# Feed-forward output product of an encoder layer: weight sums formed a product ahead, product ends in small pieces, last product closed row tile by row tile

## The chip, the core and the metric

The kernel runs on one core of one Trainium2 chip. The core has TensorE (matrix products), VectorE and ScalarE (elementwise work), GpSimd, and a sync engine whose only work here is to issue transfers. The metric is the device time of one execution in microseconds (us). The kernel before takes 2346.46 us, the median of three runs; the fastest of them took 2345.99 us and one was disturbed (10064.24 us).

## The reference

The layer has a mixer (stick-breaking attention, a spatial-gating branch and memory attention) and a feed-forward part, for 1024 prompt rows and 64 sample rows of width 1024. The change touches only the second product of the feed-forward part, the norm behind it and the residual sum:

```python
D_FF = 2816
def ffn_sublayer(x, g_pre, w_ffn_in, w_ffn_out, g_post):
    a, b = jnp.split(rmsnorm(x, g_pre) @ w_ffn_in, 2, axis=-1)
    return x + rmsnorm((jax.nn.silu(a) * b) @ w_ffn_out, g_post)
```

`rmsnorm(y, g)` divides each row by the root of its mean square and multiplies it by g, so a row of the output is final only when both of its column halves are known.

## The kernel before

All matrix products are float32 products made of three TensorE passes: each operand is split into a high part (a rounded copy, `fp32r`) and a low part (the difference), and `mm3` adds high·high, high·low and low·high.

The product `h @ w_ffn_out` (1088 x 2816 by 2816 x 1024) is done by Strassen's scheme in its seven-product form. The 2816 rows of the weight are two halves of eleven blocks of 128 rows (index k, `NK = 11`), and its 1024 columns are two halves of 512. `FO[0, k]` holds the two column halves of block k of the upper half, `FO[1, k]` those of the lower half; each is a tile `fw` of 128 x 2 x 512. The seven products are run one after the other in the order p1, p2, p3, p5, p6, p7, p4. Each takes eleven steps k. A step needs one operand pair: the weight operand W (a block of the weight, or a sum of blocks) and the activation operand A (a block of h, or a sum, which earlier code has stored in device memory as `fS` or `fA` and which is loaded into a tile `fa`). `fsplit` makes the pair W, W-low, and the pair A, A-low, in tiles `fop`: one ScalarE copy for the high part, one VectorE subtraction for the low part. So a step has two ScalarE copies and two VectorE subtractions.

With the pairs of step k, TensorE does 12 matmuls of 128 x 512 (`fout_mm`): two pairs of row tiles, `jp` 0 and 1, two row tiles each, three passes each. The sums of a `jp` stand in one two-bank tile `pb` of the accumulator memory; there are three such tiles. p1, p2, p3 and p5 have two more matmuls a step for the 64 sample rows (`fout_sample`).

In p5, p6, p7 and p4 the weight operand is itself a sum: `fout_ops` forms it in place in a `fw` tile with one more VectorE subtraction right before `fsplit` (before.py L1242 to L1249). In that step the ScalarE copy waits for the sum, and the VectorE subtraction waits for the copy.

At the end of a product `fout_post` (L1344) takes the sums out of `pb` and combines them with stored ones (tiles `p1`, `p3`, `p5`, `C11`, 128 x 2 x 512 each; the profile's views leave digits away, so that the tiles p1, p3 and p5 all read `p` there, and C11 reads `C`). After p6 the four row tiles 0 to 3 are complete in both column halves, after p7 the right halves of row tiles 4 to 7, after p4 their left halves. `scaled` (L1337) then takes a ScalarE square sum of each row tile and half (`square`, output `junk`) and multiplies by the gain `gpf` on VectorE. When both halves of a row tile have their square sums, two tiny VectorE instructions and one on GpSimd make `rstd`, and two VectorE instructions SCALAR_TENSOR_TENSOR ("puts") add the scaled halves onto the residual `x2r`, which is loaded from device memory; each is stored by a transfer.

What sets the order: the kernel is written out by hand through a planner that runs while the program is built. `get_wop(i)` writes out operand pairs up to `LA[0]` operands ahead of the one that TensorE takes (`LA_END = 4`: two steps), and their loads `RA[0]` further. Each engine executes its own list in that order. `fout_post` is written out in the step that ends the product, so the operands of steps k = 0 and 1 of the next product stand ahead of it on VectorE and those of k = 2 behind it. Small background pieces (`stream`) are taken by `breathe()` when the planner's clock of their engine is no more than `BACK[0]` us (`BACKLOG_END = 6`) ahead of TensorE's. The sync engine issues all transfers in order; a store waits there for the instruction that makes its data, and loads behind it wait too.

The last product, `fout_last` (L1399), does all eleven steps for row tiles 4 and 5 (`jp` 0, six matmuls a step), keeps the operands, and then does row tile 6 and row tile 7 with 33 matmuls each. `last_tile` finishes a row tile.

Of the kernel before, what the change touches and what calls it, by code (L numbers as in the profile page):

```python
# [15 lines left out]
P = 128  # L16
# [28 lines left out]
LA_FIN = 2  # L45
LA_END = 4
RA_END = 4

FS_GATE = [2, 9]
LA_BR = 4  # L50
# [1 line left out]
BACKLOG_ATT = 1000  # L52
BACKLOG_MEM = 6
BACKLOG_OUT = 10
BACKLOG_END = 6
X_AHEAD = 4
AHEAD = 4

# [86 lines left out]
def encoder_layer(  # L145
# [14 lines left out]
    clock, at = clocks.t, clocks.at  # L160
# [40 lines left out]
    def f32(ap):  # L201
        return ap.bitcast(F32)
# [10 lines left out]
    def act(out, in_, f=AF.Copy, **kw):  # L213
        nc.scalar.activation(out, in_, f, **kw)

    def sub(out, a, b):
        nc.vector.tensor_tensor(out, a, b, op=ALU.subtract)

    def add(out, a, b):
        nc.vector.tensor_tensor(out, a, b, op=ALU.add)  # L220

    def mul(out, a, b):
        nc.vector.tensor_tensor(out, a, b, op=ALU.mult)
# [152 lines left out]
    def get_raw(i):  # L376
        return raw_t[i]
# [827 lines left out]
    def w_raw(h, m, k):  # L1205

        def f():
            if (h, k) not in FO:
                FO[h, k] = A([P, 2, 512], F32, "fw")
            load(FO[h, k][:, m], w_ffn_out[0, (h * NK + k) * P:(h * NK + k + 1) * P, m * 512:(m + 1) * 512])  # L1210
            return FO[h, k][:, m]
        raws.append(f)
        return len(raws) - 1

    def a_raw(name, k):
        def f():
            until(lambda: (name, k) in STORED)
            x = U([P, 512], F32, "fa")
            load(x, fS[name][k])
            return x  # L1220
        raws.append(f)
        return len(raws) - 1

    def fsplit(src):
        t = A([P, 2, 512], F32R, "fop")
        act(t[:, 0], src)
        sub(t[:, 1], src, f32(t[:, 0]))
        return t

    FORM = {"p1": "A11", "p2": "A12", "p3": "S4", "p5": "S1", "p6": "S2", "p7": "S3", "p4": "A22"}  # L1230

    def fout_ops(name, k):


        new = {"p1": (0, 0), "p2": (1, 0), "p3": (1, 1), "p5": (0, 1)}
        r = [w_raw(*new[name], k)] if name in new else []
        ra = a_raw(FORM[name], k)

        def w():
            if name in ("p1", "p2", "p3"):  # L1240
                return fsplit(get_raw(r[0]))
            t, b = FO[0, k], FO[1, k]  # L1242
            x, y = {"p5": (t[:, 1], t[:, 0]), "p6": (b[:, 1], t[:, 1]), "p7": (t[:, 0], b[:, 1]),
                    "p4": (b[:, 0], b[:, 1])}[name]
            if name == "p7":
                sub(x, y, x)
            else:
                sub(x, x, y)
            return fsplit(x)  # L1249
        return wop(w, *r), wop(lambda: fsplit(get_raw(ra)), ra)  # L1250


# [43 lines left out]
    def square(j, m, src):  # L1296

        n = src.shape[0]
        ss = sm.tile([P, 1], F32, tag="ssf", name=nm("ssf"), bufs=18)[:n]
        act(U([P, 512], F32, "junk")[:n], src, AF.Square, accum_out=ss)  # L1300
        SQ.setdefault(j, {})[m] = (ss, src)
        if len(SQ[j]) == 2:
            s0, s1 = SQ[j][0][0], SQ[j][1][0]
            add(s0, s0, s1)
            SQ[j]["r"] = rstd_of(s0, D)
            n_ = n

            def ld():
                x = RES[j] = A([P, D], F32, "x2r")[:n_]
                load(x, x2sc[j * P:j * P + n_])  # L1310

            def put(m):
                src = SQ[j][m][1]
                x = RES[j][:, m * 512:(m + 1) * 512]
                nc.vector.scalar_tensor_tensor(x, src, SQ[j]["r"], x, op0=ALU.mult, op1=ALU.add)

            def out(m):
                x = RES[j][:, m * 512:(m + 1) * 512]
                store(y_prompt[0][j * P:(j + 1) * P, m * 512:(m + 1) * 512] if j < 8 else
                      y_sample[0][:, m * 512:(m + 1) * 512], x)  # L1320
            need = ("dve", lambda: max(at(RES[j], SQ[j]["r"]), at(SQ[j][0][1], SQ[j][1][1])))
            st = [x for m in range(2) for x in ((*need, lambda m=m: put(m)),
                                                ("sync", lambda: at(RES[j]), lambda m=m: out(m)))]
            if j in RES:
                stream(*st)
            else:
                stream(("sync", lambda: 0, ld), *st)
# [6 lines left out]
    def pair(pt):  # L1334
        return pt.rearrange("p (i n) -> p i n", i=2)

    def scaled(j0, m, c):  # L1337

        for i in range(2):
            square(j0 + i, m, c[:, i])  # L1340
        g = FO["g"][:, m * 512:(m + 1) * 512]
        mul(c, c, g.unsqueeze(1).to_broadcast([P, 2, 512]))

    def fout_post(name, jp, pt):  # L1344
        def new(key):
            FO[key, jp] = A([P, 2, 512], F32, key)
            return FO[key, jp]

        src = pair(pt)
        if name in ("p1", "p3"):  # L1350
            act(new(name), src)
        elif name == "p2":
            add(new("C11"), src, FO["p1", jp])
        elif name == "p5":
            act(new("p5"), src)
            c = FO["p3", jp]
            add(c, src, c)
        elif name == "p6":
            t, c = FO["p1", jp], FO.pop(("p3", jp))
            add(t, src, t)  # L1360
            add(c, c, t)
            scaled(2 * jp, 0, FO.pop(("C11", jp)))
            scaled(2 * jp, 1, c)
        elif name == "p7":
            t, c = FO["p1", jp], FO.pop(("p5", jp))
            add(t, src, t)
            add(c, c, t)
            scaled(4 + 2 * jp, 1, c)

    def last_tile(j, pt):  # L1370
        u = FO["p1", j // 2][:, j % 2]
# [27 lines left out]
    def fout_last():  # L1399

        kept = []

        def first(k, ws):
            def f(tiles):
                w, a = tiles
                kept.append((w, a))
                if k == 0:
                    fill(psum_free("b"))
                    FO["pt", 0] = PB()
                fill(at(w, a))  # L1410
                fout_mm(FO["pt", 0], a, w, 0, (0, 1), k)
                breathe()
                if k == NK - 1:
                    for j in range(2):
                        last_tile(j, FO["pt", 0])
            steps.append((ws, f))

        def rest(j):
            def f(tiles):
                if j == 2:  # L1420
                    fill(psum_free("b"))
                    FO["pt", 1] = PB()
                res_early(4 + j)
                for k, (w, a) in enumerate(kept):
                    fout_mm(FO["pt", 1], a, w, 1, (j,), k)
                    if k % 3 == 2:
                        breathe()
                last_tile(j, FO["pt", 1])
            steps.append(([], f))
        for k in range(NK):  # L1430
            first(k, fout_ops("p4", k))
        for j in (2, 3):
            rest(j)

    for name in ("p1", "p2", "p3", "p5", "p6", "p7"):
# [609 lines left out]
```

## Time and profile before

| what | before |
|---|---|
| median of the runs shown | 2346.46 us |
| the profiled execution's own time | 2345.06 us |
| its span, first to last instruction | 2343.1 us |
| TensorE busy / weight loads busy | 95% / 92% of the span |
| VectorE busy / ScalarE busy | 68% / 33% |
| mean granted clock of TensorE | 0.986 of full speed |
| start of p6 (its first matmul) | 2204.18 us |
| end of the last matmul | about 2335.5 us |

The profile is one execution. Times are microseconds from the start of the span. PE is TensorE's matmuls, PEld its weight loads, DVE VectorE, ACT ScalarE, POOL GpSimd, SP the sync engine. PEclk is the granted TensorE clock as a share of 2.4 GHz. A matmul's end is modelled, so the starts are the better measure. In the timeline, a row of TensorE merges matmuls that follow each other, and the bracket says how long the engine stood idle ahead of it, and what ended that.

### The profile page before, as it was taken

How to read it: one execution, taken by the hardware profiler on the slowest of the kernel's cores; microseconds unless marked ns; L12 is line 12 of the kernel's file. 1: busy time of each engine (PE TensorE's matmuls, PEld its weight loads, DVE VectorE, ACT ScalarE, POOL GpSimd, SP SyncE). 2: the span in 40 equal slices, each digit the busy share in tenths (PEclk: the TensorE clock that was granted, in tenths of full speed). 3: DMA queues.
4: the chain of work that ended last, by engine and by line, in shares of the span. 5: the costliest groups of instructions: out<-in, count | busy, mean ns of one | idle time of the engine just before them, and what ended most of it. 6: DMA issues, size and time to landing. Idle time of an engine off the chain costs nothing.

```text
span 2343.1 us, 40746 instructions
## 1 busy us (share of the span) xinstructions
PE 2229.2 (95%) x16465; PEld 2146.5 (92%) x16465; DVE 1602.8 (68%) x2473; ACT 783.3 (33%) x1383; POOL 141.8 (6%) x236
## 2 busy tenths in 40 slices
PE   7899999999999999988899999988999999999986
PEld 6899999999999998877799999987999999988764
DVE  7856688867776665699934354488777777764676
ACT  8432222332222224667612122243121112143442
POOL 2000000000000000243200000221000000000000
PEclk9999999999999999999999999999999999999998
DMA  6532356755582236845435251341332323265242
GB/s 203 180 98 99 129 198 220 233 181 197 174 293 97 95 126 247 308 159 206 130 121 160 95 168 65 109 131 64 115 92 83 101 92 112 80 238 190 82 148 85
DMA packets 249535, 345.97 MB, mean 148 GB/s; under 512 B 17140, under 2 KB 184644, under 8 KB 249348
## 3 DMA queue, kind: packets, MB, share of 16 engines
q1 hardware_dynamic: 249348, 343.38, 43.6%
q8 instruction: 130, 2.13, 0.4%
q14 instruction: 57, 0.47, 0.1%
HBM read 222.54 MB, written 120.78 MB: 147 GB/s over the span
## 4 chain that ended last, share of the span: by engine, by line
PE 43%; DVE 5%; ACT 1%; issue 1%; DMA 1%; POOLq 0%; DVEq 0%; SPq 0%; ACTq 0%
PE pb L73 41%; PE pt L73 2%; DVE fop L73 1%; ACT fop L73 1%; DVE fw L73 1%; DVE p L73 1%; DVE bt L73 1%; DMA raw<-in_w_ffn_in_dram 0%; DVE x2r L73 0%; ACT junk L73 0%; DVE whl L73 0%; DMA fa<-fS 0%; DVE XhT2a L73 0%; DVE t L73 0%; DVE XhT2b L73 0%
## 5 line engine op out<-in xcount | busy, mean ns | idle before, releaser
L73 DVE TENSOR_TENSOR c<-pb,u 128x544 f32<-128x544 f32 (+2 forms) x236 | 168.2, 713 | 245.2 <-PE pb L73 233.0
L73 ACT ACTIVATE whl<-raw 128x512 fp32r<-128x512 f32 x254 | 157.2, 634 | 461.5 <-PE pb L73 200.6
L73 PE MATMUL pb<-fop,fop 128*128 128x512 f32 x924 | 230.7, 400 | 26.6 <-ACT fop L73 22.7
L73 PEld LDWEIGHTS pb<-fop,fop 128*128 128x128 f32 x924 | 174.6, 191 | 75.2 <-ACT fop L73 29.6
L73 DVE TENSOR_TENSOR whl<-raw,whl 128x512 fp32r<-128x512 f32 x286 | 193.2, 690 | 10.0 <-ACT whl L73 8.9
L73 DVE TENSOR_TENSOR u<-pb,u 128x544 f32<-128x544 f32 (+2 forms) x177 | 125.5, 709 | 66.4 <-PE pb L73 66.4
L73 DVE TENSOR_TENSOR whl<-u,whl 128x512 fp32r<-128x512 f32 x232 | 160.0, 690 | 6.0
L73 PE MATMUL pb<-XhB21a,whl 128*128 128x288 f32 x656 | 144.9, 296 | 0.0
L73 PE MATMUL pb<-XhB11a,whl 128*128 128x288 f32 x656 | 144.7, 296 | 0.0
L73 PE MATMUL pb<-XhB22a,whl 128*128 128x288 f32 x656 | 144.2, 295 | 0.0
L73 PE MATMUL pb<-XhB11b,whl 128*128 128x256 f32 x656 | 131.7, 284 | 0.0
L73 PE MATMUL pb<-XhB21b,whl 128*128 128x256 f32 x656 | 131.6, 284 | 0.0
L73 PE MATMUL pb<-XhB22b,whl 128*128 128x256 f32 x656 | 131.1, 283 | 0.0
L73 ACT ACTIVATE c<-c 128x1088 f32<-128x1088 f32 x38 | 42.4, 1115 | 227.7 <-DVE c L73 227.7
L73 PEld LDWEIGHTS pb<-XhB11a,whl 128*128 128x128 f32 x656 | 109.8, 188 | 0.0
L73 PEld LDWEIGHTS pb<-XhB22a,whl 128*128 128x128 f32 x656 | 109.8, 188 | 0.0
L73 PEld LDWEIGHTS pb<-XhB21a,whl 128*128 128x128 f32 x656 | 109.7, 188 | 0.0
L73 PE MATMUL pb<-Xrh,whl 128*128 128x288 f32 (+1 forms) x512 | 101.9, 294 | 6.9 <-DVE whl L73 6.9
L73 PEld LDWEIGHTS pb<-XhB21b,whl 128*128 128x128 f32 x656 | 107.6, 191 | 0.0
L73 PEld LDWEIGHTS pb<-XhB22b,whl 128*128 128x128 f32 x656 | 107.5, 191 | 0.0
L73 PEld LDWEIGHTS pb<-XhB11b,whl 128*128 128x128 f32 x656 | 107.2, 190 | 0.1
L73 PE MATMUL pb<-XhT1a,whl 128*128 128x288 f32 x464 | 102.1, 296 | 1.0 <-DVE sgo L73 1.0
(327 smaller groups left out, 6373.1 us busy)
## 6 DMA issues: line engine op xcount, KB each, us to landing
raw<-in_w_in_dram SPq DMA_DIRECT2D x72, 512.0 KB
raw<-in_w_ffn_in_dram SPq DMA_DIRECT2D x88, 256.0 KB
gsc<-c SPq DMA_DIRECT2D x24, 544.0 KB
grow<-gsc SPq DMA_DIRECT2D x24, 544.0 KB
raw<-in_w_branch_dram SPq DMA_DIRECT2D x24, 512.0 KB
fS<-fsum SPq DMA_DIRECT2D x44, 256.0 KB
fw<-in_w_ffn_out_dram SPq DMA_DIRECT2D x44, 256.0 KB
fa<-fS SPq DMA_DIRECT2D x44, 256.0 KB
```

Of the source, the lines that this page charges most:

```text
L73: r = fn(*a, **k)
```

## The change

The weight sums leave the step that uses them. A table `SUMS` gives each sum a place in an earlier step: those of p5 one every second step in p2 and p3, those of p6 in p5's steps, those of p7 from p5's step 6 to p6's step 5, those of p4 from p6's step 6 to p7's step 5. In such a step the sum stands between the ScalarE copy and the VectorE subtraction of the weight operand (`between`). The loads of the weight quarter that p5 uses move to the same steps of p2 and p3.

At the ends of p6 and p7, `scaled` becomes a chain of background pieces for one row tile each (the add, the square, the multiplication), and so do the adds that combine the sums; only the instructions that empty `pb` stay where they were. `BACKLOG_END` goes from 6 to 4.

The last product takes both `jp` in the steps k = 0 to 5, keeps the operands of k = 6 to 10, with ten operands written out ahead (`LA_LAST`), and then finishes the row tiles 4 to 7 one after the other with 15 matmuls each. The four residual loads are written out ahead of them.

```diff
+LA_LAST = 10
+LAST_K = 6
-BACKLOG_END = 6
+BACKLOG_END = 4
...
-    def fsplit(src):
+    def fsplit(src, between=lambda: None):
         t = A([P, 2, 512], F32R, "fop")
         act(t[:, 0], src)
+        between()
         sub(t[:, 1], src, f32(t[:, 0]))
...
+    SUMS = {}
+    for k in range(NK):
+        for n, name in ((NK + 2 * k + 1, "p5"), (3 * NK + k, "p6"), (3 * NK + 6 + k, "p7"), (4 * NK + 6 + k, "p4")):
+            SUMS.setdefault(n, []).append((name, k))
...
-    def scaled(j0, m, c):
-
+    def scaled(j0, m, c, make=None):
+        g = FO["g"][:, m * 512:(m + 1) * 512]
         for i in range(2):
-            square(j0 + i, m, c[:, i])
-        g = FO["g"][:, m * 512:(m + 1) * 512]
-        mul(c, c, g.unsqueeze(1).to_broadcast([P, 2, 512]))
+            st = [("act", lambda: at(c), lambda i=i: square(j0 + i, m, c[:, i])),
+                  ("dve", lambda: at(c), lambda i=i: mul(c[:, i], c[:, i], g))]
+            if make:
+                st.insert(0, ("dve", lambda: at(c), lambda i=i: make(i)))
+            stream(*st)
...
             add(t, src, t)
-            add(c, c, t)
             scaled(2 * jp, 0, FO.pop(("C11", jp)))
-            scaled(2 * jp, 1, c)
+            scaled(2 * jp, 1, c, lambda i: add(c[:, i], c[:, i], t[:, i]))
...
+                if k == 0:
+                    LA[0] = LA_LAST
+                if k >= LAST_K:
+                    kept.append((w, a))
+                    return
+                for jp in range(2):
...
+        for j in range(4):
+            steps.append(([], lambda tiles, j=j: res_early(4 + j)))
+        for j in range(4):
             rest(j)
```

VectorE at the end of p6 and the start of p7. Before: the end of p6's post work for the second pair of row tiles and the operands behind it; `fw_2985` and `fw_2990` are the weight sums of p7's steps 2 and 3, the `fop` rows the low parts of W and A.

```order
L73 TENSOR_TENSOR p1_3045_23177<-pb_3173_24002,p1_3045_23177 128x1024
L73 TENSOR_TENSOR p3_3130_23710<-p3_3130_23710,p1_3045_23177 128x1024
L73 TENSOR_TENSOR C11_3091_23446<-C11_3091_23446,gpf_3172_24000 128x1024
L73 TENSOR_TENSOR ssf_3213_24245<-ssf_3213_24245,ssf_3217_24252 128x1
L73 TENSOR_SCALAR rstd_3219_24256<-ssf_3213_24245 128x1
L73 TENSOR_TENSOR ssf_3215_24248<-ssf_3215_24248,ssf_3220_24259 128x1
L73 TENSOR_SCALAR rstd_3222_24263<-ssf_3215_24248 128x1
L73 TENSOR_TENSOR p3_3130_23710<-p3_3130_23710,gpf_3172_24000 128x1024
L73 TENSOR_TENSOR p1_3046_23185<-pb_3174_24009,p1_3046_23185 128x1024
L73 TENSOR_TENSOR p3_3131_23718<-p3_3131_23718,p1_3046_23185 128x1024
L73 TENSOR_TENSOR C11_3092_23454<-C11_3092_23454,gpf_3172_24000 128x1024
```

The next rows before are four tiny ones, one more product with `gpf`, and then the sum and the two subtractions of step 2. In the changed kernel the same place, from the row that empties `pb` to the operands of step 2 (`fop_3217`, `fop_3219`); `fw_3063` is a weight sum of p4, not of p7:

```order
L75 TENSOR_TENSOR p1_3045_23180<-pb_3173_24018,p1_3045_23180 128x1024
L75 TENSOR_TENSOR C11_3091_23459<-C11_3091_23459,gpf_3172_24016 128x512
L75 TENSOR_TENSOR p3_3130_23728<-p3_3130_23728,p1_3045_23180 128x512
L75 TENSOR_TENSOR p1_3046_23188<-pb_3174_24025,p1_3046_23188 128x1024
L75 TENSOR_TENSOR p3_3130_23728<-p3_3130_23728,p1_3045_23180 128x512
L75 TENSOR_TENSOR C11_3092_23467<-C11_3092_23467,gpf_3172_24016 128x512
L75 TENSOR_TENSOR p3_3131_23736<-p3_3131_23736,p1_3046_23188 128x512
L75 TENSOR_TENSOR fw_3063_23271<-fw_3063_23271 128x512
L75 TENSOR_TENSOR fop_3217_24278<-fw_2985_22850,fop_3217_24278 128x512
L75 TENSOR_TENSOR fop_3219_24284<-fa_3208_24227,fop_3219_24284 128x512
```

Ahead of step 2's operands there stood eight rows of full width and eight tiny ones, and now there are two of full width and five of half width; the other pieces have moved behind the operands of steps 2 to 10.

TensorE in the last product. Before, its steps for one `jp` and the start of row tile 6 (`pb_3312`):

```order
L73 MATMUL pb_3283_24581<-fop_3302_24679,fop_3303_24682 128x512 x6
L73 MATMUL pb_3283_24581<-fop_3304_24692,fop_3305_24695 128x512 x6
L73 MATMUL pb_3312_24734<-fop_3266_24513,fop_3268_24518 128x512 x3
L73 MATMUL pb_3312_24734<-fop_3269_24534,fop_3271_24539 128x512 x3
L73 MATMUL pb_3312_24734<-fop_3280_24573,fop_3282_24578 128x512 x3
```

In the changed kernel step 5 for both `jp` (`pb_3275`, `pb_3276`), and then row tile 4 with the kept operands of steps 6 to 10:

```order
L75 MATMUL pb_3275_24581<-fop_3284_24614,fop_3285_24617 128x512 x6
L75 MATMUL pb_3276_24588<-fop_3284_24614,fop_3285_24617 128x512 x6
L75 MATMUL pb_3275_24581<-fop_3286_24620,fop_3288_24625 128x512 x3
L75 MATMUL pb_3275_24581<-fop_3289_24640,fop_3291_24645 128x512 x3
L75 MATMUL pb_3275_24581<-fop_3298_24670,fop_3300_24675 128x512 x3
L75 MATMUL pb_3275_24581<-fop_3301_24692,fop_3302_24695 128x512 x3
L75 MATMUL pb_3275_24581<-fop_3303_24711,fop_3304_24714 128x512 x3
```

A step that had six matmuls has twelve, and the rows behind the steps are groups of 15 for one row tile in place of 33.

## Rows read from the trace of the kernel before

**Rows 1.** Windows: us, busy time (instructions) of each engine, PEclk, DMA share, GB/s
```profile
2099.20:2134.10 34.90, 34.90 (x155) 28.91 (x155) 15.01 (x23) 16.46 (x29) 0.00 (x0) 1.00 0.53 189
...
2169.00:2204.20 35.20, 35.20 (x157) 29.13 (x157) 20.82 (x33) 14.84 (x25) 0.00 (x0) 1.00 0.20 60
2204.20:2238.80 34.60, 34.37 (x143) 26.22 (x141) 25.25 (x41) 15.77 (x29) 0.92 (x1) 1.00 0.29 92
2238.80:2282.50 43.70, 33.38 (x130) 25.33 (x130) 36.06 (x57) 16.74 (x37) 3.69 (x4) 0.92 0.53 181
2282.50:2318.80 36.30, 21.01 (x63) 12.06 (x62) 25.54 (x36) 14.18 (x28) 0.00 (x0) 0.81 0.20 73
2318.80:2335.50 16.70, 15.92 (x69) 12.50 (x67) 8.69 (x18) 2.17 (x6) 2.76 (x3) 1.00 0.38 126
```

**Rows 2.** Timeline of TensorE, p6 to p4: start, us, engine, instruction, [idle before <-releaser]
```profile
2204.18 2.88 PE L73 MATMUL pb<-fop,fop 128*128 128x512 f32 x12
2206.91 1.88 PE L73 MATMUL pb<-ys,sel 128*128 128x512 f32 x4
2208.22 30.61 PE L73 MATMUL pb<-fop,fop 128*128 128x512 f32 x126
2240.89 4.37 PE L73 MATMUL pb<-fop,fop 128*128 128x512 f32 x18 [2.06 <-DVE p L73]
2252.15 16.68 PE L73 MATMUL pb<-fop,fop 128*128 128x512 f32 x60 [6.89 <-ACT fop L73]
...
2296.51 7.19 PE L73 MATMUL pb<-fop,fop 128*128 128x512 f32 x18 [10.66 <-ACT fop L73]
...
2327.72 7.80 PE L73 MATMUL pb<-fop,fop 128*128 128x512 f32 x33 [0.78 <-DVE p L73]
```

**Rows 3.** Waits of TensorE from 2204.2 on: total us, times, longest
```profile
PE pb L73 <- ACT fop L73: 22.7, 11, 10.7
PE pb L73 <- DVE p L73: 2.8, 2, 2.1
```

**Rows 4.** Timeline of VectorE in one step of p6
```profile
2213.54 0.69 DVE L73 TENSOR_TENSOR fop<-fw,fop 128x512 fp32r<-128x512 f32 x1 [0.70 <-ACT fop L73]
...
2214.14 0.68 DVE L73 TENSOR_TENSOR fop<-fa,fop 128x512 fp32r<-128x512 f32 x1
2214.75 0.74 DVE L73 SCALAR_TENSOR_TENSOR x2r<-yc,rstd,x2r 64x512 f32<-64x512 f32 x1
...
2215.41 0.68 DVE L73 TENSOR_TENSOR fw<-fw,fw 128x512 f32<-128x512 f32 x1
...
2216.79 0.69 DVE L73 TENSOR_TENSOR fop<-fw,fop 128x512 fp32r<-128x512 f32 x1 [0.70 <-ACT fop L73]
```

**Rows 5.** Timeline of VectorE behind p6
```profile
2240.87 1.23 DVE L73 TENSOR_TENSOR p<-p,p 128x1024 f32<-128x1024 f32 x1
...
2242.01 1.22 DVE L73 TENSOR_TENSOR C<-C,gpf 128x1024 f32<-128x1024 f32 x1
...
2248.83 0.16 DVE L73 TENSOR_TENSOR ssf<-ssf,ssf 128x1 f32<-128x1 f32 x1
...
2249.03 0.15 DVE L73 TENSOR_SCALAR rstd<-ssf 128x1 f32<-128x1 f32 x1
2249.10 1.22 DVE L73 TENSOR_TENSOR p<-p,gpf 128x1024 f32<-128x1024 f32 x1
2250.23 0.68 DVE L73 TENSOR_TENSOR fw<-fw,fw 128x512 f32<-128x512 f32 x1
```

**Rows 6.** Timeline at the end: the last row tile on VectorE
```profile
2335.55 0.69 DVE L73 TENSOR_TENSOR p<-pb,p 128x512 f32<-128x512 f32 x1 [4.11 <-PE pb L73]
...
2338.47 1.42 DVE L73 SCALAR_TENSOR_TENSOR x2r<-p,rstd,x2r 128x512 f32<-128x512 f32 x2 [0.44 <-POOL rstd L73]
```

**Rows 7.** Chain that ended last, in order of time: start, us, what
```profile
2201.17 2.72 PE pb L73 x12
...
2261.41 4.01 DMA fa<-fS
```

More of the change, by code (lines that the diff above doesn't have):

```diff
@@ L1230, in encoder_layer, with w_sum, between @@
     FORM = {"p1": "A11", "p2": "A12", "p3": "S4", "p5": "S1", "p6": "S2", "p7": "S3", "p4": "A22"}
+    FSTEPS = [(name, k) for name in FORM for k in range(NK)]
+    NEW = {"p1": (0, 0), "p2": (1, 0), "p3": (1, 1)}
+    PLACE = {"p1": (0, 0), "p2": (1, 0), "p3": (1, 1), "p5": (0, 1), "p6": (1, 1), "p7": (0, 0), "p4": (1, 0)}
+    def w_sum(name, k):
+        t, b = FO[0, k], FO[1, k]
+        if name == "p5":
+            sub(t[:, 1], t[:, 1], t[:, 0])
+        elif name == "p6":
+            sub(b[:, 1], b[:, 1], t[:, 1])
+        elif name == "p7":
+            sub(t[:, 0], b[:, 1], t[:, 0])
+        else:
+            sub(b[:, 0], b[:, 0], b[:, 1])
+    SUMS = {}
+    for k in range(NK):
+        for n, name in ((NK + 2 * k + 1, "p5"), (3 * NK + k, "p6"), (3 * NK + 6 + k, "p7"), (4 * NK + 6 + k, "p4")):
+            SUMS.setdefault(n, []).append((name, k))
     def fout_ops(name, k):
-        new = {"p1": (0, 0), "p2": (1, 0), "p3": (1, 1), "p5": (0, 1)}
-        r = [w_raw(*new[name], k)] if name in new else []
+        n = FSTEPS.index((name, k))
+        r = [w_raw(*NEW[name], k)] if name in NEW else []
         ra = a_raw(FORM[name], k)
+        sums = SUMS.get(n, [])
+        r += [w_raw(0, 1, i) for p, i in sums if p == "p5"]
         def w():
[L1240 to L1249, printed above, removed]
+            h, m = PLACE[name]
+            def between():
+                for p, i in sums:
+                    w_sum(p, i)
+            return fsplit(FO[h, k][:, m], between)
         return wop(w, *r), wop(lambda: fsplit(get_raw(ra)), ra)
@@ L1366, in fout_post @@
             add(t, src, t)
-            add(c, c, t)
-            scaled(4 + 2 * jp, 1, c)
+            scaled(4 + 2 * jp, 1, c, lambda i: add(c[:, i], c[:, i], t[:, i]))
     def last_tile(j, pt):
@@ L1405, in f @@
                 w, a = tiles
-                kept.append((w, a))
                 if k == 0:
[L1408 to L1415, printed above, removed]
+                    LA[0] = LA_LAST
[4 more added lines that the diff above has]
+                    if k == 0:
+                        fill(psum_free("b"))
+                        FO["pt", jp] = PB()
+                    fill(at(w, a))
+                    fout_mm(FO["pt", jp], a, w, jp, (2 * jp, 2 * jp + 1), k)
+                    breathe()
             steps.append((ws, f))
@@ L1419, in f @@
             def f(tiles):
[L1420 to L1423, printed above, removed]
+                pt = FO["pt", j // 2]
                 for k, (w, a) in enumerate(kept):
[L1425 to L1428, printed above, removed]
+                    fout_mm(pt, a, w, j // 2, (j,), LAST_K + k)
+                last_tile(j, pt)
+                breathe()
             steps.append(([], f))
@@ L1431, in fout_last @@
             first(k, fout_ops("p4", k))
-        for j in (2, 3):
+        for j in range(4):
+            steps.append(([], lambda tiles, j=j: res_early(4 + j)))
+        for j in range(4):
             rest(j)
```

## The prediction

> **What bounds the kernel now.** I read the windows by product first [rows 1]. Up to 2204.2 us TensorE is busy all the time at full clock: p2 takes 34.9 us and p5 35.2 us, with VectorE at 15.0 and 20.8 us, so neither the products p1 to p5 nor anything ahead of them has time to give. Behind 2204.2, in p6, p7 and p4, TensorE is busy 34.4 of 34.6, 33.4 of 43.7 and 21.0 of 36.3 us, and its granted clock falls to 0.92 and 0.81, which means that it ran for a part of these stretches at 1.2 in place of 2.4 GHz. So the change can only pay in the last 139 us.
>
> How much is there? Twelve matmuls follow each other in 2.72 us at full clock [rows 7], 0.2267 us each. p6, p7 and p4 have 3 x 132 = 396 of them, 89.8 us, and the sample rows' two matmuls with `sel` take 2208.22 - 2206.91 = 1.3 us [rows 2]: 91.1 us. From p6's first matmul at 2204.18 to the last one's end at about 2335.5 it took 131.3 us. The difference is 40.2 us, and 25.5 of these are whole waits of TensorE: 22.7 us for operands and 2.8 us for VectorE emptying or reading `pb` [rows 3]. The other 14.7 us are matmuls at the lower clock and short waits inside a step: the 18 matmuls from 2296.51 on took 7.19 us where 18 x 0.2267 are 4.1 [rows 2].
>
> Then I read why the operands are late. Behind p6 and behind p7 TensorE waits 6.89 and 10.66 us [rows 2]: it has used the two steps that stand ahead of the product's post work on VectorE, and the third step's pair stands behind all of it. Inside the steps VectorE needs 2.6 us for three subtractions that by themselves take 1.8: the low part of W waits 0.70 us for the copy, which has waited for the sum [rows 4]. That is hardly less than TensorE's 2.72 us, so VectorE never gets ahead again.
>
> **Prices.** VectorE's instructions follow each other faster than they last, and the starts give what one costs: 0.605 us for half width (2213.54, 2214.14, 2214.75), 0.66 for a put (2214.75 to 2215.41) [rows 4], 1.14 for full width (2240.87 to 2242.01), 0.27 for a pair of tiny ones (2248.83 to 2249.10) [rows 5]. By their durations they would be 0.685, 0.745, 1.22 and 0.31. I take the starts, since these rows stand back to back as the new ones will; the durations are the other end.
>
> **p2 to p5.** Eleven sums are added to p2 and p3 and eleven loads of 256 KB move there; p5 loses its eleven own sums and gets sixteen others. VectorE is busy 15.0 of 34.9 us in p2 and gets 3.4 us more. p5 has 38 subtractions, 23 us, in 35.2. The sum now stands where VectorE waited for the copy. I take nothing for this: the cover is TensorE's full 35 us a product. `BACKLOG_END` moves no row of an engine ahead of the second product in the written order, and costs nothing. So p6 begins at 2204.2 as before.
>
> **p6.** A step is now 3 x 0.605 = 1.8 us on VectorE with no wait in it, against 2.72. Steps 3 and 4 still stand behind the sample rows' post work, which ends at the same time as before; their pairs come just as TensorE needs them, and I take 0.3 us. p6 ends at 2208.2 + 120 x 0.2267 + 0.3 = 2235.7, its `jp` 0 at 2234.4.
>
> **p7.** Counted from that 2234.4, TensorE has 1.4 us of `jp` 1 and 5.4 us of steps 0 and 1, so it comes to step 2 at 6.8 and needs the low part of A by 7.25. VectorE empties `jp` 0 (1.14), does two half-width rows, empties `jp` 1 (1.14), does three more, and then the sum and the two low parts: the last ends at 7.3. So the wait of 6.89 us shrinks to nothing, and that of 2.06 us, for `pb`, goes as well, since VectorE is ahead when `jp` 0 ends. After it, with the background pieces in the order in which they stand: step 3 is ready at 9.7 against 10.0, step 4 at 12.4 against 12.7, step 5, behind two products with the gain, a put and a tiny pair, at 16.4 against 15.4. That is a wait of 0.9 us. From step 7 on no sum is left and VectorE gains: step 10 is ready at 28.8 against 29.5. I take 1.0 us; the bounds are 0 (every piece fits) and 5.8, below. p7 ends at 2235.7 + 29.9 + 1.0 = 2266.6.
>
> **p4.** VectorE is free for p7's end 1.0 us after its `jp` 0. It empties twice with one add behind each (3.5 us) and has step 2 ready 1 us before TensorE comes to it, where 10.66 us were waited. A step is then two subtractions, 1.21 us, and even with four more pieces step 10 is ready 2 us before row tile 4 needs it. ScalarE needs two copies a step, less than VectorE. Left are the waits for row tiles that share a two-bank tile: before, the last row tile began 0.78 us late, after VectorE had read its neighbour's sums [rows 2]. The new order has this twice, at row tiles 5 and 7, and the written order has a wait for VectorE there: 1.6 us. The Trainium skill (PSUM — Partial Sum Buffer, Summary: rules for kernel authors) asks a reader to keep to another bank than the running matmul, and the two row tiles lie in two banks, so by it no wait is needed and the sum would be 1.6 us less. I go by the row, which shows the wait. p4 ends at 2266.6 + 29.9 + 1.6 = 2298.1, all at full clock, since no wait over 1 us is left.
>
> **The end.** From the last matmul to the end of the span it was 2343.1 - 2335.5 = 7.6 us [rows 6]. The chain of add, square, `rstd` and puts stays, but VectorE is still at the puts of the row tiles before when the last one ends (0.2 us), and between the last two puts stands one of another row tile (0.66 us): 8.5 us. The four residual loads stand behind the last operand load, some 10 us ahead of their first use, against 4 us that a load took [rows 7], and cost nothing.
>
> **The sum.** The span becomes 2298.1 + 8.5 = 2306.6 against 2343.1: 36.5 us less. The profiled execution took 2.0 us more than its span (2345.06), and the median is 1.4 us above that: **2310.0 us**, 1.6% less than 2346.46.
>
> **The rivals.** (1) VectorE becomes the bound of p7. From p6's `jp` 0 to p7's it has 2 full-width, 38 half-width, 8 puts and 4 tiny pairs: 31.6 us by the starts, which is already more than TensorE's 29.9, and 35.7 by the durations, 5.8 us over. For it speaks that in the same stretch before it was busy 36.1 us [rows 1]; against it that rows back to back start faster than they last. It decides when each piece costs its duration or waits for another engine: then p7 is 5.8 us late and p4's steps start with up to 3 us more, 2316 to 2319. Chance 0.18. The Trainium skill (Perfetto Trace Analysis, Optimizing Scalar/DVE Operations) says that larger operations help where an engine is saturated, and smaller ones where it only makes bubbles elsewhere. The ten full-width rows that are split here cost 0.7 us more by the starts and 1.5 us by the durations, which are in these sums. (2) The sync engine. Stores now stand between the operand loads, each waiting for its put, and a load behind them starts only then. The tightest is p4's step 0: its load may start 22 us after p6's `jp` 0 and is needed at 29, and a load took 4.0 us [rows 7]. It decides when landing takes over 7 us; three loads late by 2 us give 2316. Chance 0.09. (3) Slower than before: VectorE executes in order, and the eleven sums in p2 and p3 wait for weight quarters just loaded. Their loads are written out two steps ahead, 6.3 us. To eat the 36.5 us, each would have to stop TensorE for 3.3 us, so land 9.6 us after its issue, against 4.0 seen and with the transfer engines at 0.53 in p2 [rows 1]: 2347 and more. Chance 0.02. (4) The ten operands ahead in p4 don't come, since they wait for tiles that TensorE still reads. Row tile 4 takes a pair each 0.68 us, and VectorE makes one each 1.21: 5 x 0.53 = 2.7 us, 2313. Chance 0.05, and inside the forecast's neighbourhood.
>
> **Chances.** The forecast's own course has 0.61 and lies within 2306 to 2313. Below it is little: with no wait at all the span is 2204.2 + 91.1 + 7.6 = 2302.9 and the time 2306.3, so less than 2306 has 0.03; another 0.02 goes to times over 2319 for causes not named. The range is 2306 to 2319: the forecast, rival 4, and rivals 1 and 2 to their upper prices. What this kernel's measurement can tell from no change is taken as 2%, 47 us, more than the 40 us that TensorE loses there at all. So a time lower by over 2% has 0.02, one higher by over 2% 0.02, and within 2% lies 0.96, although I expect a clear step down inside it.
>
> **What would show it.** Right: p6 starts at 2204 still; no wait of TensorE over 2 us behind p6 or p7; a granted clock of 1.00 in both; p6, p7 and p4 some 31.5, 31 and 31.5 us long; two waits of 0.8 us for VectorE in the last four row tiles; the last matmul near 2298. Wrong: VectorE busy without a gap through p7 with TensorE waiting for operands in many steps (rival 1), copies waiting for `fa` loads (rival 2), or sums in p2 and p3 behind a load (rival 3).

## The result, and the profile after

The changed kernel takes 2309.87 us (median of four runs, 2308.90 to 2311.32) against 2346.22 us (the median of four, one of them disturbed; without it 2345.99); the ratio of the undisturbed runs is 0.9847, with a 95% interval of 0.9827 to 0.9866. Forecast was 2310.0.

The windows by product, as in [rows 1] (us, busy time and instructions of PE, PEld, DVE, ACT, POOL, then PEclk, DMA share, GB/s); the rows are p2, p5, p6, p7, p4 and the end:

```profile
2099.20:2134.10 34.90, 34.90 (x155) 28.93 (x155) 19.18 (x30) 16.27 (x30) 0.00 (x0) 1.00 0.66 234
...
2169.00:2204.20 35.20, 35.20 (x157) 29.15 (x157) 24.43 (x39) 14.59 (x26) 0.00 (x0) 1.00 0.20 61
2204.20:2235.70 31.50, 31.50 (x137) 25.41 (x136) 26.30 (x45) 18.26 (x36) 2.12 (x1) 1.00 0.42 127
2235.70:2266.60 30.90, 30.63 (x133) 24.50 (x132) 30.73 (x56) 15.16 (x32) 3.68 (x4) 1.00 0.63 211
2266.60:2298.10 31.50, 29.75 (x129) 23.61 (x127) 23.96 (x44) 12.64 (x29) 2.76 (x3) 1.00 0.38 135
2298.10:2306.30 8.20, 0.00 (x0) 0.00 (x0) 4.11 (x8) 0.72 (x2) 0.86 (x1) 0.66 0.51 195
```

TensorE is now busy at the full clock in all three products, where p7 and the stretches behind it had 0.92 and 0.81. VectorE does 4.2 us more in p2 and 3.6 more in p5, and TensorE still has no gap in either window. In p7 VectorE has no gap any more: 30.73 of 30.9 us.

TensorE's timeline (start, us, engine, instruction, [idle before <- releaser]), which answers to [rows 2], and its waits from 2204.2 on (total us, times, longest), which answer to [rows 3]:

```profile
2202.83 2.88 PE L75 MATMUL pb<-fop,fop 128*128 128x512 f32 x12
2205.55 1.88 PE L75 MATMUL pb<-ys,sel 128*128 128x512 f32 x4
2206.86 41.95 PE L75 MATMUL pb<-fop,fop 128*128 128x512 f32 x181
2248.98 36.50 PE L75 MATMUL pb<-fop,fop 128*128 128x512 f32 x158 [0.17 <-DVE fop L75]
2286.26 7.14 PE L75 MATMUL pb<-fop,fop 128*128 128x512 f32 x30 [0.78 <-DVE p L75]
2294.18 3.74 PE L75 MATMUL pb<-fop,fop 128*128 128x512 f32 x15 [0.78 <-DVE p L75]
```

```profile
PE pb L75 <- DVE p L75: 1.6, 2, 0.8
PE pb L75 <- DVE fop L75: 0.2, 1, 0.2
```

The waits of 2.06, 6.89 and 10.66 us are gone; 25.5 us of waiting became 1.8. What is left on this list is one short wait in p7 and two ahead of row tiles 5 and 7.

VectorE behind p6, which answers to [rows 5], from the row that empties `pb` for the first pair of row tiles to step 2's operands, and at step 5's:

```profile
2233.35 1.22 DVE L75 TENSOR_TENSOR p<-pb,p 128x1024 f32<-128x1024 f32 x1 [3.16 <-PE pb L75]
2234.49 0.68 DVE L75 TENSOR_TENSOR C<-C,gpf 128x512 f32<-128x512 f32 x1
2235.09 0.68 DVE L75 TENSOR_TENSOR p<-p,p 128x512 f32<-128x512 f32 x1
...
2239.24 0.68 DVE L75 TENSOR_TENSOR fop<-fw,fop 128x512 fp32r<-128x512 f32 x1
2239.84 0.69 DVE L75 TENSOR_TENSOR fop<-fa,fop 128x512 fp32r<-128x512 f32 x1
...
2246.97 0.75 DVE L75 SCALAR_TENSOR_TENSOR x2r<-C,rstd,x2r 128x512 f32<-128x512 f32 x1
...
2248.84 0.69 DVE L75 TENSOR_TENSOR fop<-fa,fop 128x512 fp32r<-128x512 f32 x1
```

VectorE waits 3.16 us for TensorE here, so it is ahead at p6's end. Step 2's pair is ready 7.2 us after 2233.35 (12.5 in the run with the post work whole, below). The rows start 0.60 and 1.14 us apart although they last 0.68 and 1.22.

**A measure for effects near 1 us.** From p2's end (the row on VectorE that fills C11, 2132.76 before, 2131.40 after) to p6's first matmul it takes 71.42 us before and 71.43 after. Ahead of p2's end the kernels are alike, apart from the sums and loads in p2, and yet p6's first matmul stands between 2202.83 and 2207.62 us in the profiled runs below; 2205.35 in a second run of the changed kernel. So single microseconds are read in the profiled runs, one of each kernel, from p6's first matmul on, in four stages (the two profiled runs of the changed kernel agree within 0.02 us in each): to the row that empties `pb` for p6's first pair, to the same row of p7, to the add of the last row tile, and to the end. TensorE alone would need 132 x 0.2267 = 29.92 us for the second stage and 138 x 0.2267 = 31.28 for the third.

| kernel | median, us | p6 | p7 | p4 | end | sum |
|---|---|---|---|---|---|---|
| before | 2346.22 | 35.44 | 44.88 | 51.05 | 7.55 | 138.92 |
| changed | 2309.87 | 30.52 | 31.47 | 33.14 | 8.34 | 103.47 |
| changed, second run | 2310.30 | 30.52 | 31.47 | 33.12 | 8.34 | 103.45 |
| sums in their own step | 2339.94 | 35.49 | 36.96 | 42.26 | 18.98 | 133.69 |
| post work whole | 2325.00 | 30.53 | 37.19 | 40.39 | 9.04 | 117.15 |
| former last product | 2311.90 | 30.53 | 31.48 | 35.63 | 7.49 | 105.13 |
| sums alone | 2326.08 | 30.52 | 37.21 | 41.96 | 7.49 | 117.18 |
| row tiles 4, 6, 5, 7 | 2308.75 | 30.53 | 31.47 | 31.89 | 8.26 | 102.15 |
| one-bank tiles | 2310.03 | 30.53 | 31.48 | 31.97 | 8.30 | 102.28 |
| p4's sums early | 2309.60 | 30.53 | 30.00 | 33.52 | 9.09 | 103.14 |
| nine rows more | 2314.27 | 30.53 | 36.23 | 32.38 | 8.32 | 107.46 |
| pieces of full width | 2311.56 | 30.53 | 31.73 | 33.49 | 9.02 | 104.77 |
| planner's lead 6 us | 2312.24 | 30.52 | 32.99 | 33.49 | 9.06 | 106.06 |
| three edits together | 2307.99 | 30.53 | 29.92 | 31.88 | 7.70 | 100.03 |

### The profile page after: what moved, and what is told of

It reads as the page before. It is cut to its first block, busy times and chain, and to the rows that moved or that the text cites. A ratio compares the mean times of both kernels' runs of the same rounds, so it can differ in the third digit from the quotient of the medians.

```text
span 2306.3 us, 40728 instructions
## 1 busy us (share of the span) xinstructions
PE 2218.2 (96%) x16465; PEld 2144.9 (93%) x16465; DVE 1600.3 (69%) x2483; ACT 781.4 (34%) x1383; POOL 143.8 (6%) x236
## 5 line engine op out<-in xcount | busy, mean ns | idle before, releaser
L75 PE MATMUL pb<-fop,fop 128*128 128x512 f32 x924 | 219.3, 391 | 1.9 <-DVE p L75 1.6
```

The source lines that it names most:

```text
L75: r = fn(*a, **k)
```

## The experiments

### Which part brings how much: one part undone, or one alone

**Sums in their own step**

```diff
-            def between():
-                for p, i in sums:
-                    w_sum(p, i)
-            return fsplit(FO[h, k][:, m], between)
...
+            if name == "p7":
+                sub(x, y, x)
+            else:
+                sub(x, x, y)
+            return fsplit(x)
```

> The changed kernel with one part undone: the weight sums stand again in the step that uses them, ahead of the copy. The theory (a step of p6, p7 and p4 costs VectorE 1.8 us with the sum made ahead and 2.6 us with the sum and the wait for the copy, against TensorE's 2.72): VectorE again never gets ahead, the background pieces push operands back in p7 and p4, and more than half of the 36.5 us is lost: 2325 to 2335 us, with waits of TensorE for operands in many steps of p7 and p4 and a granted clock under 1.00 there. The rival (the post work at the products' ends is what counts, the sums are a side matter): 2310 to 2315 us.

Here the planner finds so little room on VectorE that one background add of p6 stands behind the row of p7 that overwrites its operand `p1`, and adds of p7 stand behind rows of p4 that do. VectorE's rows are the same in kind and number, but part of the layer's output is made from wrong numbers, so only the time of this run is used. The time is 2339.94 us, ratio 0.9975 (0.9966 to 0.9985): 30.2 of the 35.4 us are lost, and the time lies past the upper end of what was expected. VectorE in two steps of p7:

```profile
2253.42 0.69 DVE L75 TENSOR_TENSOR fop<-fw,fop 128x512 fp32r<-128x512 f32 x1 [0.76 <-ACT fop L75]
...
2254.63 0.69 DVE L75 TENSOR_TENSOR fw<-fw,fw 128x512 f32<-128x512 f32 x1
2256.01 0.69 DVE L75 TENSOR_TENSOR fop<-fw,fop 128x512 fp32r<-128x512 f32 x1 [0.70 <-ACT fop L75]
```

The step's period is 2256.01 - 2253.42 = 2.59 us, with the wait of [rows 4] back. The stages p6, p7 and p4 lose 5.0, 5.5 and 9.1 us. What the expectation missed is the end: pieces for which no step had room pile up behind the last product, 10.6 us more. TensorE's longest wait is 2.6 us, and its clock 1.00 in p6 and p7, 0.88 in p4.

**Post work whole**

```diff
-            stream(*st)
...
+        mul(c, c, g.unsqueeze(1).to_broadcast([P, 2, 512]))
...
+            add(c, c, t)
...
-BACKLOG_END = 4
+BACKLOG_END = 6
```

> The changed kernel with the post work of p6 and p7 written out whole again (full-width adds and products with the gain, squares in the same place) and the planner's lead back at 6 us. The theory: VectorE has 8 full-width rows and the tiny ones, some 10 us, ahead of the operands of p7's step 2, which it then ends 12.0 us after p6's first pair of row tiles, where TensorE needs them at 7.25: a wait of 4.8 us behind p6, some 1 to 3 us behind p7, and 2 to 4 us more by a clock that falls in the waits: 2316 to 2322 us. The rival (the sums made ahead are enough, since VectorE is then 1.4 us ahead at the product's end and catches up): under 2313 us, with no wait over 2 us.

2325.00 us, ratio 0.9910 (0.9895 to 0.9925): 13.7 us in the stages, 5.7 in p7, 7.25 in p4, 0.7 at the end. TensorE behind p6 and behind p7, and the windows of these two stages:

```profile
2246.20 0.80 PE L75 MATMUL pb<-fop,fop 128*128 128x512 f32 x1 [3.46 <-ACT fop L75]
2247.88 32.05 PE L75 MATMUL pb<-fop,fop 128*128 128x512 f32 x131 [0.88 <-DVE fop L75]
2283.20 17.89 PE L75 MATMUL pb<-fop,fop 128*128 128x512 f32 x63 [3.27 <-ACT fop L75]
```

```profile
2235.98:2273.17 37.19, 32.84 (x133) 26.14 (x132) 31.37 (x51) 16.02 (x34) 3.62 (x4) 0.91 0.57 196
2273.17:2313.56 40.39, 35.49 (x138) 27.23 (x136) 24.90 (x39) 14.20 (x32) 2.75 (x3) 0.92 0.20 70
```

The waits behind p6, 3.46 and 0.88 us by their brackets, stand where 4.8 us were worked out. Behind the waits the granted clock fell, to a mean of 0.91 and 0.92 in the two stages: 131 matmuls behind the first took 32.05 us where 131 x 0.2267 are 29.7, and 63 behind the second 17.89 where 14.3 would do. These 6 us, where 2 to 4 were taken, put the time above the range: the stages alone would give 2309.87 + 13.7 = 2323.6 us, and the other 1.4 us of the median stand in no stage.

**Former last product**

```diff
-                for jp in range(2):
+                fout_mm(FO["pt", 0], a, w, 0, (0, 1), k)
...
+                    fout_mm(FO["pt", 1], a, w, 1, (j,), k)
```

> The changed kernel with the last product in its former order: eleven steps of six matmuls for row tiles 4 and 5, then row tiles 6 and 7 with 33 each. The theory: a step takes TensorE 1.36 us and VectorE 1.21 us for two subtractions, and p7's post work and the background pieces (3.5 us and up to 10 us) have to go in between, so TensorE waits 4 to 8 us in the first eleven steps; one wait of 0.78 us and 0.9 us of the end are saved: 2313 to 2318 us. The rival (the order matters only through its own waits for row tiles): 2308.5 us.

2311.90 us, ratio 0.9856 (0.9839 to 0.9872), between the two readings. TensorE in p4:

```profile
2271.80 4.77 PE L75 MATMUL pb<-fop,fop 128*128 128x512 f32 x18 [0.47 <-DVE fop L75]
2277.83 16.66 PE L75 MATMUL pb<-fop,fop 128*128 128x512 f32 x68 [1.25 <-DVE fop L75]
2295.28 7.80 PE L75 MATMUL pb<-fop,fop 128*128 128x512 f32 x33 [0.78 <-DVE p L75]
```

The short steps do make TensorE wait, but 0.47 and 1.25 us, not 4 to 8: p4 is 2.5 us longer and the end 0.85 shorter. The new order is worth 1.7 us by the stages.

**Sums alone**

```diff
+            def between():
+                for p, i in sums:
+                    w_sum(p, i)
```

> The kernel before with one part of the change alone: the weight sums made a product ahead. The theory: the waits inside the steps go, but the post work still stands whole ahead of p7's step 2 and of p4's step 2, and the last product's short steps cannot hide it: 2320 to 2328 us, so about half of the gain by this part alone, and the three parts together give about what they give one by one. The rival (the parts help only together): over 2335 us.

2326.08 us, ratio 0.9917 (0.9902 to 0.9932): 21.7 of the 35.4 us, as expected. It has the same sum as the run with whole post work, 117.18 against 117.15, so the new last product alone brings nothing while the post work still stands whole: it gains 1.6 us in p4 and gives 1.55 back at the end. That the parts add up was expected and is wrong. They overlap: taken away one by one they cost 30.2, 13.7 and 1.7 us, together 45.6 of 35.4. Without the sums the pieces find no room.

### Is VectorE the bound of p7?

The changed kernel was run a second time, and beside it with less and with more work for VectorE in p7.

> The changed kernel once more, unaltered, as the measure for the three runs beside it: 2309.9 us, within 1.2 us.

It came out at 2310.30 us, ratio 0.9850 (0.9833 to 0.9868).

**p4's sums early**

```diff
-..., (4 * NK + 6 + k, "p4")):
+..., ((3 * NK + 1 if k < 5 else 4 * NK) + k, "p4")):
```

> The changed kernel, with p4's weight sums made earlier: five in p5's steps 1 to 5 and six in p6's steps 5 to 10, none in p7. VectorE has 3.6 us less to do in p7, where it is busy 30.7 of 30.9 us, and 3 us more in p5, where it is busy 24.4 of 35.2. If VectorE's row of work is what delays p7's step 5 and the steps around it, TensorE's 1.8 us of stalls in p6 and p7 fall to under 0.8 and the time by 1 to 1.5 us. If VectorE is a full bound of p7 (rival 1), the time falls by more, up to 3.6 us. If the stalls have another cause (copies, loads), nothing changes.

**Nine rows more**

```diff
                 for p, i in sums:
                     w_sum(p, i)
+                if name == "p7" and k >= 2:
+                    sub(FO["x"], FO[h, k][:, m], FO[1, k][:, 1])
```

> The changed kernel, with one more half-width subtraction on VectorE in each of p7's steps 2 to 10, whose result nobody reads: nine rows, 5.4 us by the starts. If VectorE is the bound of p7 (it is busy 30.7 of 30.9 us there), TensorE is late by nearly as much: 4 to 6 us more, 2314 to 2316. If most of that busy time is background work which can go on in p4 (VectorE is busy 24 of 31.5 us there), a step with its extra row still takes 2.4 us against 2.72, and the time rises by under 2 us.

2309.60 us (ratio 0.9848, 0.9832 to 0.9864) and 2314.27 us (0.9875, 0.9857 to 0.9892). The stage p7 in three kernels: p4's sums early, changed, nine rows more:

```profile
2236.99:2266.99 30.00, 30.00 (x133) 24.69 (x132) 29.02 (x53) 13.97 (x29) 3.68 (x4) 1.00 0.64 217
```

```profile
2233.35:2264.82 31.47, 31.20 (x135) 24.95 (x134) 31.33 (x56) 15.14 (x31) 3.68 (x4) 1.00 0.58 193
```

```profile
2234.07:2270.30 36.23, 34.43 (x144) 26.34 (x142) 36.09 (x64) 16.40 (x33) 2.95 (x4) 1.00 0.47 163
```

VectorE's busy time (the third pair of numbers) is 29.02 of 30.00, 31.33 of 31.47 and 36.09 of 36.23 us. With 5.4 us more work p7 lengthens by 4.76 us, though TensorE's own 29.92 us are the same; with 3.6 us less it falls to 30.00, TensorE's own time, and not lower. So VectorE is the bound of p7 in the changed kernel, by 1.5 us, and TensorE comes next right below it. Of these 1.5 us, 1.1 are waits of TensorE: the 339 matmuls from behind `sel` to row tile 4 take 78.62 us in the changed kernel (2206.86 to 2285.48), and with p4's sums early they stand in one row of 77.53:

```profile
2210.50 77.53 PE L75 MATMUL pb<-fop,fop 128*128 128x512 f32 x339
```

The other 0.4 us is VectorE coming late to p7's first sums, and p4 gets it back. With nine rows more the second reading, that background work would give way and go on in p4, falls: only 0.76 us of the 4.76 came back there.

The early sums gain just 0.3 us in all, where 1 to 1.5 were expected: of the 1.47 us in p7, p4 takes 0.38 back and the end 0.75. With VectorE's list ordered anew, five puts stand behind the last `rstd` where there were four. The last rows of VectorE, changed kernel and p4's sums early:

```profile
2297.96 0.69 DVE L75 TENSOR_TENSOR p<-pb,p 128x512 f32<-128x512 f32 x1
...
2300.30 2.73 DVE L75 SCALAR_TENSOR_TENSOR x2r<-p,rstd,x2r 128x512 f32<-128x512 f32 x4
```

```profile
2300.51 0.69 DVE L75 TENSOR_TENSOR p<-pb,p 128x512 f32<-128x512 f32 x1
...
2302.91 3.39 DVE L75 SCALAR_TENSOR_TENSOR x2r<-p,rstd,x2r 128x512 f32<-128x512 f32 x5
```

**Planner's lead 6 us**

```diff
-BACKLOG_END = 4
+BACKLOG_END = 6
```

> The changed kernel, with the planner's lead for background pieces (BACKLOG_END) at 6 us again. In p7 the pieces then stand a step or two earlier: the add of the second row tile ahead of step 3's operands and the first put ahead of step 4's. If VectorE's order around p7's steps 3 to 5 decides TensorE's stalls, they grow by 0.5 to 2 us: 2310.5 to 2312. If only the sum of VectorE's work in p7 counts, the time is that of the changed kernel within 0.5 us.

2312.24 us (ratio 0.9853, 0.9838 to 0.9868). p7 and p4 together last 66.48 us against 64.61, so 1.9 us more, and the end 0.7 more, again with five puts. VectorE's work in p7 is nearly the same (31.41 us busy against 31.33); what counts besides its sum is what stands ahead of the operands:

```profile
2249.32 6.17 PE L75 MATMUL pb<-fop,fop 128*128 128x512 f32 x24 [0.54 <-DVE fop L75]
2256.03 33.76 PE L75 MATMUL pb<-fop,fop 128*128 128x512 f32 x146 [0.54 <-DVE fop L75]
```

**Pieces of full width**

```diff
...
-        for i in range(2):
-            st = [("act", lambda: at(c), lambda i=i: square(j0 + i, m, c[:, i])),
-                  ("dve", lambda: at(c), lambda i=i: mul(c[:, i], c[:, i], g))]
+        st = [("act", lambda: at(c), lambda i=i: square(j0 + i, m, c[:, i])) for i in range(2)]
+        st.append(("dve", lambda: at(c), lambda: mul(c, c, g)))
...
```

> The changed kernel, with the post work of p6 and p7 still made of background pieces, but of full width: one add and one product with the gain for both row tiles of a pair in place of two each. If it is the moving behind the operands that pays, the time stays within 1 us of the changed kernel's 2310: ten rows of 1.14 us replace twenty of 0.605, 0.7 us less work for VectorE in p7 and p4, against up to 0.5 us more that an operand can wait for a piece. If the splitting pays (an operand pair must not stand behind 1.14 us), TensorE waits in several steps of p7 and the time rises by 2 us or more.

2311.56 us (ratio 0.9852, 0.9836 to 0.9869): 0.6 us more in p7 and p4 together and 0.7 at the end, five puts once more; the stages' sum is 1.3 us higher, between the two readings. So it is the moving, with the planner's lead at 4 us, that pays 13.7 us, and the splitting at most 1.3, of which 0.7 is the order of the puts. The Trainium skill (Perfetto Trace Analysis, Optimizing Scalar/DVE Operations) says that grouping work can improve throughput where an engine is saturated. VectorE is busy 31.33 of 31.47 us in p7, and grouping did spare it 0.5 us from p6's start to the end (85.82 against 86.33 us busy); the stages p7 and p4 still grew by 0.6 us with the coarser pieces.

### The waits between row tiles

**Row tiles 4, 6, 5, 7**

```diff
-        for j in range(4):
+        for j in (0, 2, 1, 3):
             rest(j)
```

> The changed kernel, with the last four row tiles of p4 finished in the order 4, 6, 5, 7 in place of 4, 5, 6, 7, so that two that follow each other never share a two-bank tile. If the two waits of 0.78 us come from the shared tile, both vanish and the time falls by 1.6 us, to 2308.3, with the tail as long as before. If they come from something else (VectorE reading any accumulator memory, or a row tile's operands), they stay, and the time is that of the changed kernel within 0.3 us.

**One-bank tiles**

```diff
...
-                        FO["pt", jp] = PB()
+                        FO["pt", jp] = PB() if jp else [PT(), PT()]
...
```

> The changed kernel, with the sums of p4's row tiles 4 and 5 in two tiles of one bank each in place of the two halves of one two-bank tile; row tiles 6 and 7 share a two-bank tile as before, and no row of any engine moves. If the wait of 0.78 us belongs to the shared tile, and not to two banks being written and read at once, row tile 5 begins without a wait and row tile 7 still waits 0.78 us: from p6's first matmul to the end 102.7 us in place of 103.46, the time 2309.3. If TensorE has to wait whenever VectorE reads sums that it has just made, both waits stay and the time is that of the changed kernel.

2308.75 us (ratio 0.9849, 0.9833 to 0.9864) and 2310.03 us (0.9843, 0.9830 to 0.9856). TensorE in the order 4, 6, 5, 7, and with one-bank tiles for row tiles 4 and 5 (`pt`):

```profile
2251.80 46.70 PE L75 MATMUL pb<-fop,fop 128*128 128x512 f32 x203 [0.17 <-DVE fop L75]
```

```profile
2286.70 6.96 PE L75 MATMUL pt<-fop,fop 128*128 128x512 f32 x30
2293.50 3.56 PE L75 MATMUL pb<-fop,fop 128*128 128x512 f32 x15
2297.85 3.72 PE L75 MATMUL pb<-fop,fop 128*128 128x512 f32 x15 [0.78 <-DVE p L75]
```

Both waits vanish in the one, and only that of row tile 5 in the other, where the two banks are in two tiles, and VectorE reads one while TensorE writes its neighbour. So the wait belongs to the shared tile. The Trainium skill (PSUM — Partial Sum Buffer, Summary: rules for kernel authors) asks a reader to target a different bank from that of the running matmul, and this run agrees: with a tile for each bank, row tile 5 begins without a wait. In the median the one-bank tiles show no gain (2310.03 against 2309.87 and 2310.30): this profiled run reached p6 only at 2207.62.

A wait costs more than its bracket. With it, 15 matmuls lie 4.52 us apart on VectorE's reads, without it 3.40:

```profile
2285.52 0.69 DVE L75 TENSOR_TENSOR p<-pb,p 128x512 f32<-128x512 f32 x1 [3.17 <-PE pb L75]
2290.04 0.69 DVE L75 TENSOR_TENSOR p<-pb,p 128x512 f32<-128x512 f32 x1 [0.77 <-PE pb L75]
2293.44 0.69 DVE L75 TENSOR_TENSOR p<-pb,p 128x512 f32<-128x512 f32 x1 [0.91 <-PE pb L75]
```

That is 1.12 us for a bracket of 0.78, and p4 with one-bank tiles is shorter by 33.14 - 31.97 = 1.17 us. The other 0.34 us has two halves. A listed end is 0.16 us late: 12 matmuls are listed with 2.88 us at 2202.83, and the next begins 2.72 us on. The Trainium skill (Perfetto Trace Analysis, Tensor Engine Instruction) calls this end an estimate of the profiler, and the trace agrees. And a row behind such a wait is longer: 30 matmuls take 7.14 us behind one and 6.96 without, 15 take 3.72 and 3.56. In the order 4, 6, 5, 7 the two waits are 2.24 us less, but p4 is shorter by only 1.25: the last add begins 1 us late, since VectorE is at three puts until 2299.5:

```profile
2297.55 2.07 DVE L75 SCALAR_TENSOR_TENSOR x2r<-p,rstd,x2r 128x512 f32<-128x512 f32 x3
...
2299.54 0.68 DVE L75 TENSOR_TENSOR p<-pb,p 128x512 f32<-128x512 f32 x1
```

### Three edits together

```diff
+        if j == 3:
+            until(lambda: sum(x[0] == "dve" for st in streams for x in st) <= 2)
         add(u, pt[:, (j % 2) * 512:(j % 2) * 512 + 512], u)
+        if j == 3:
+            until(lambda: sum(x[0] == "dve" for st in streams for x in st) <= 1)
...
+                BACK[0] = 1000
...
+        for j in (0, 2, 1, 3):
```

(and p4's sums early, as above; `BACK[0]` is the planner's lead, lifted for the last four row tiles)

> The changed kernel with three edits: p4's sums made in p5 and p6 (as in the run with early sums), the last row tiles in the order 4, 6, 5, 7 (as in the run with that order), and the puts of the other row tiles taken out of the end: two of them are written in the gaps in which VectorE waits for the last row tile's square sum and its rstd, so that two puts follow that rstd in place of four or five. From p6's first matmul to the end of the span the changed kernel takes 103.46 us; less 1.1 (stalls of p6 and p7), 1.56 (the two waits) and 0.7 (one put) it is 100.1, and the time 2306.9 us. If the gains do not add up, since VectorE's work only moves into p4 and to the end, 2308 to 2309.

2307.99 us (2305.68 to 2308.94), ratio 0.9834 (0.9819 to 0.9848). The stages sum to 100.03 us, 3.4 less than the changed kernel and what was worked out; p7 is at TensorE's 29.92. In the medians only 1.9 and 2.3 us of it show, against the two runs of the changed kernel, so the time lies where it was expected if the gains did not add up, and the interval overlaps that of the changed kernel. This profiled run reached p6 only at 2206.47. The end:

```profile
2210.51 87.66 PE L75 MATMUL pb<-fop,fop 128*128 128x512 f32 x384
```

```profile
2297.47 1.41 DVE L75 SCALAR_TENSOR_TENSOR x2r<-p,rstd,x2r 128x512 f32<-128x512 f32 x2
2298.80 0.69 DVE L75 TENSOR_TENSOR p<-pb,p 128x512 f32<-128x512 f32 x1
2299.40 0.74 DVE L75 SCALAR_TENSOR_TENSOR x2r<-p,rstd,x2r 128x512 f32<-128x512 f32 x1
...
2301.19 2.07 DVE L75 SCALAR_TENSOR_TENSOR x2r<-p,rstd,x2r 128x512 f32<-128x512 f32 x3
```

TensorE runs 384 matmuls without a listed wait, and three puts follow the last `rstd`. The last add is still 0.6 us late, behind two puts.

## Why the prediction was right, step by step

**What bounds the kernel.** Right. 35.4 of the 40.2 us that TensorE lost behind 2204.2 us came back, p6, p7 and p4 run at full clock, and p2 to p5 pay nothing for VectorE's added work (4.2 us in p2 where 3.4 were taken, and 24.4 us busy in p5 where 23 were).

**p6.** The number fits, but by luck: 0.3 us of stall was taken, and none came. The stage lasts 30.52 or 30.53 us in all twelve kernels with the sums made ahead, also with p4's sums early, where the 339 matmuls behind `sel` stand in one row of 77.53 us: 339 x 0.2267 = 76.85, 0.16 of a listed end, and 0.5 more. Most of that stands at `sel`: the first matmul behind it is listed with 0.79 us, in the kernel before as in the changed one, where one lasts 0.39. So the two matmuls with `sel` cost about 0.4 us more than the 1.3 that were taken, and the operands of steps 3 and 4 cost nothing.

**p7.** Right in size and in reason. 1.0 us taken, 1.1 measured (78.62 against 77.53, above). Step 2's pair ended 7.2 us after p6's first pair was emptied, against 7.3, and step 5's operands were late as foretold (ready at 16.2 against 16.4). VectorE gained behind step 7, too: step 10's pair ends at 28.5 against 28.8, and behind step 5 TensorE lists no wait in p7. (By the prediction's own terms TensorE needs that pair at 16.3 + 5 x 2.72 = 29.9, not 29.5, which changes nothing.)

```profile
2261.15 0.68 DVE L75 TENSOR_TENSOR fop<-fa,fop 128x512 fp32r<-128x512 f32 x1
```

Rival 1's mechanism was there as well: VectorE had no gap until it emptied p7's first pair, 31.47 us after p6's, which is the 31.6 us that rival 1 gave as VectorE's sum by the starts, and the run with nine rows more shows that it is the bound. Only its price by the durations, 35.7 us, did not come. The prediction already held that VectorE would come to p7's sums late, by 1.0 us; it came about 0.4 us late, and TensorE lost nothing by it.

**p4.** The step that was mis-sized: two waits of 0.78 us as foretold, but they cost 2.24 us in place of 1.6, since the bracket understates a wait. The starts were there to be read: in the kernel before, VectorE reads row tile 6's sums at 2326.97 and row tile 7's at 2335.55 [rows 6], 8.58 us for 33 matmuls of together 7.48, so the wait cost 1.10.

```profile
2326.97 0.69 DVE L73 TENSOR_TENSOR p<-pb,p 128x512 f32<-128x512 f32 x1 [0.62 <-PE pb L73]
```

**The end.** 8.34 us from the last add against 7.55 before, so 0.79 more, where 0.86 were taken: one put of 0.66 and small change. The 0.2 us for a busy VectorE did not come (it was free when the last row tile ended), but another order makes it 0.6 to 1.0.

**The sum.** From p6's first matmul on 102.4 us were predicted and 103.47 measured: 0.64 more by the two waits, 0.1 each in p6 and p7, and 0.16 because the matmuls were added up by their starts and the end was counted from a listed end; the rest is rounding. That this does not show in the total is luck: p6 began at 2202.83 in this run in place of 2204.2, and runs differ there by more.

**The other rivals.** Rival 2 (loads behind stores) shows its sign, not its price: from 2204.2 us on ScalarE waits 7.8 us for five loads of p4's `fa`, and 4.4 us for the first of them, still in p7. It waited for none of them before. TensorE waits for no such load, and VectorE has no gap in p7, so nothing is lost here:

```profile
ACT fop L75 <- DMA fa<-fA: 7.8, 5, 4.4
```

Rival 3 did not come (p2 and p3 last 34.9 us as before). Rival 4 did not either: TensorE lists no wait for operands at row tile 4.

**What was not asked.** The prediction gave no price to `BACKLOG_END` in p7. It is worth 2.6 us with the pieces (0.7 of it at the end), by the order in which VectorE gets its rows.

## What to carry to other kernels

Where an engine that prepares operands is near its limit, first take the waits out of its steps (make the sum that a copy needs a stage earlier), then move what is not urgent behind the next operands: the second pays little before the first has made room (without the sums made ahead, the rest of the change brought the stages from 138.92 to 133.69 us), and the room is found by adding VectorE's rows by their starts and comparing with TensorE's time for the same stretch. Pieces that are deferred can pile up at the end of the kernel and must not outlive their operands. Price a short wait of TensorE by the starts on both sides, not by its bracket, and give neighbouring banks tiles of their own where one is read while the other is written.

## What the runs showed that had not been expected

- A wait of TensorE with a bracket of 0.78 us costs 1.12 us in the changed kernel (4.52 against 3.40 us for 15 matmuls) and 1.10 in the kernel before.
- The order of VectorE's last pieces moves the end by 0.7 us, and edits that shift the planner's clocks can reorder them: four puts behind the last `rstd` in the changed kernel, two in the kernel before, five in four of the runs.
- The stretch up to p2's end, in which no run here changes more than loads and sums of p2, ends between 2131.40 and 2136.20 us in the profiled runs, 4.8 us apart. What makes it vary was not tried.
